# Chunk 4's last weight sum on VectorE instead of an accumulating DMA, and the residual written into PSUM by ScalarE ahead of the products

## The chip, the cores and the metric

The kernel runs on one core of a Trainium2 chip. The metric is the device time of one execution in microseconds (us). The engines are called PE (TensorE, matrix products), DVE (VectorE), ACT (ScalarE), POOL (GpSimd) and SP (SyncE, which only issues DMAs here). A profile is taken of one further execution, in which each instruction's start and duration are recorded.

## The reference

Two layers over 256 tokens of width 1024, float32 throughout. Each layer applies four residual steps, each followed by a layer norm with its own gain and bias:

```
x = layer_norm(x * ALPHA + 0.5 * swiglu(x, ffn1_gate, ffn1_up, ffn1_down))
x = layer_norm(x * ALPHA + mixer(x))          # gated conv, recurrence, pooling; w_in, w_out
x = layer_norm(x * ALPHA + cross_attn(x, mem, ca_q, ca_k, ca_v, ca_o))
x = layer_norm(x * ALPHA + 0.5 * swiglu(x, ffn2_gate, ffn2_up, ffn2_down))

swiglu(x, g, u, d) = (silu(x @ g) * (x @ u)) @ d       # g, u: 1024 x 2816, d: 2816 x 1024
```

ALPHA is a constant, the fourth root of 4. The comments name what each step holds; the mixer itself is not touched by the change.

## The kernel before

The tokens lie in two tiles of 128 (h, 128 x 1024 each); x transposed (xT) is PE's stationary or moving operand. Each weight is loaded as float32 into a 128 x 1024 buffer (raw, six of them), and split in two parts that PE multiplies at its fast rate: ACT rounds it to a high part (whi, L75), DVE subtracts to get the low part (wlo, L76). The eight buffers of each part turn over. A product is then three matmuls (mm_rows, L132): high by high, low by high, high by low.

A swiglu (called net here) has 2816 hidden columns, worked in five chunks of 512 (0 to 4) and one of 256 (5). For each, gate and up products go to PSUM banks of the kind acc; the hidden values are then gated, dealt to the other layout by small DMAs (dealt) and multiplied with the down weights, which adds up in four PSUM banks of the kind dn (two token tiles by two halves of the columns), over the whole net.

Some chunks, the sevens, compute the gate and up products by seven block products in place of eight (by_seven, L663 on): in the first net chunks 2 and 4, in the other three 2, 3, 4 and 5. For these, blocks of the weights are w00 and w10 (gate, first and second half of the rows) and w01 and w11 (up). The seven products take w00, w00 + w01, w10, w00 + w01 + w11, w01 + w11, w11 and last w00 + w01 + w11 + w10. Each sum that grows from w00 is made in w00's buffer in place. A sum by DVE is an instruction at L702 (raw<-raw). The last sum, to which w10 is added, is made before the change in two ways. For chunks of 512 (chunk 4 among them) POOL issues two accumulating DMAs, 512 KB each (the function more, L738), which read w10 from memory once more and add it to the buffer. For chunk 5 DVE adds w10's buffer. The sum w01 + w11 uses accumulating DMAs as well and stays as it is. At the end of a seven, DVE takes the bank called total into the hidden values (halves, L721); the last product of chunk 4 then writes that same bank, and so waits for it.

The homes of the blocks: w10 of a 512 chunk lies in spare2 and one raw buffer; chunk 5's w00 takes spare2 next. SP issues all plain loads in one queue in an order fixed by the scheduler, and an issue whose buffer is still in use holds up all behind it. lng and lnb are the norm's gain and bias, whose buffers sevens use as homes too.

At the end of each step finish (L328 on) makes for each tile the residual: h = h * ALPHA / scale + dn in two halves by DVE (L377, with the row sum as second result where the norm follows by ACT's squares), then the mean (L387), ACT's sum of squares (L392), rs (L398), the two norm operations (L407, L412) and PE's transposes (L199) for the next step.

Of the kernel before, what the change touches and what calls it, by code (L numbers as in the profile page):

```python
# [60 lines left out]
def model(ctx: ExitStack, tc: tile.TileContext, t: dict, out: bass.AP):  # L61
# [99 lines left out]
    def tok(i):  # L161
        return slice(i * P, (i + 1) * P)
# [162 lines left out]

    squares = kTh[:, 4:8, :].rearrange("p k c -> p (k c)")

    def finish(mm, y, scale, gb, units, last=False, junk=None, ahead=None, prompt=False):  # L328

        g, b = gb
        def later_split(i, j, unit):
            pt = acc((P, 4, P))
            for k in range(4):
                turns.append(nc.tensor.transpose(pt[:, k, :], h[i][:, (4 * j + k) * P : (4 * j + k + 1) * P], unit))
            dh, dl = (x[:, 4 * j : 4 * j + 4, tok(i)] for x in (xTh, xTl))
            nc.scalar.copy(dh, pt)  # L340
            return dh, dl, pt

        def turn_first():
            if prompt:
                held.extend(later_split(0, j, units[0]) for j in range(2))
            else:
                transposed(h[0], 0, xTh, xTl, units[0])

        def low_part(w):
            lows.append(nc.vector.tensor_tensor(w[1], w[2], w[0].bitcast(F32), op=ALU.subtract))  # L350

        held = []

        def tile_done(i):

            st = sm.tile([P, 4, 6], F32, tag="st", name="st")
            pieces, size = [slice(0, 512), slice(512, DM)], 512
            if last and i == NT - 1:

                pieces, size = [slice(0, 512), slice(512, 768), slice(768, DM)], 256  # L360
                c = slice(512, DM)
                v = halves(h[i][:, c])
                with tc.issue_after(lows[-1].ins):
                    nc.vector.scalar_tensor_tensor(v, v, ALPHA / scale, sums(y[i][1]), op0=ALU.mult, op1=ALU.add)
            for c in pieces:
                n = c.start // 512
                v = halves(h[i][:, c])
                if len(pieces) == 3 and n:
                    o = acc((P, 256))
                    mm(i, n, slice(c.start - 512, c.stop - 512), o, None)  # L370
                    nc.vector.tensor_tensor(v, v, sums(o), op=ALU.add)
                else:
                    mm(
                        i, n, slice(0, 512), None,
                        None if last or not i or not n else turn_first,
                    )
                    nc.vector.scalar_tensor_tensor(  # L377
                        v, v, ALPHA / scale, sums(y[i][n]), op0=ALU.mult, op1=ALU.add,
                        accum_out=None if junk is None else st[:, n, 0:1],
                    )  # L380
                for d in range(c.start, c.stop, size):
                    if junk is None:
                        nc.vector.bn_stats(st[:, d // size, :], h[i][:, d : d + size])
            mv = sm.tile([P, 2], F32, tag="mv", name="mv")
            rs = sm.tile([P, 1], F32, tag="rs", name="rs")
            if junk is not None:
                mean = nc.vector.tensor_scalar(  # L387
                    mv[:, 0:1], st[:, 0, 0:1], st[:, 1, 0:1], -1.0 / DM, op0=ALU.add, op1=ALU.mult
                )
                with ExitStack() as behind:  # L390
                    squared.append(
                        nc.scalar.activation(junk, h[i], AF.Square, bias=mv[:, 0:1], accum_out=mv[:, 1:2])  # L392
                    )
                    if prompt:
                        with tc.issue_after(mean.ins):
                            low_part(held.pop(0))
                        behind.enter_context(tc.issue_after(lows[-1].ins))
                    nc.vector.tensor_scalar(  # L398
                        rs, mv[:, 1:2], 1.0 / DM, LN_EPS / scale / scale, op0=ALU.mult, op1=ALU.add
                    )  # L400
            else:
                nc.vector.bn_aggr(mv, st[:, 0 : DM // size, :])
                nc.vector.tensor_scalar_add(rs, mv[:, 1:2], LN_EPS / scale / scale)
            nc.gpsimd.tensor_tensor(rs, rs, nhalf[:, 0:1], op=ALU.pow)
            cs = [slice(0, 512), slice(512, DM)]
            for c in cs:
                nc.vector.scalar_tensor_tensor(  # L407
                    h[i][:, c], h[i][:, c], mv[:, 0:1], g[:, c],
                    op0=ALU.subtract if junk is None else ALU.add, op1=ALU.mult,
                )  # L410
            for c in pieces:
                normed.append(nc.vector.scalar_tensor_tensor(  # L412
                    h[i][:, c], h[i][:, c], rs, b[:, c], op0=ALU.mult, op1=ALU.add
                ))
                if last:
                    e = nc.scalar if c.start == 512 else nc.sync
                    e.dma_start(out[0, tok(i), c], h[i][:, c])

        if ahead is None:
            tile_done(0)  # L420
            tile_done(1)
        else:
            split(*ahead.todo[0])
            if prompt:
                nc.scalar.copy(ahead.todo[1][0], ahead.todo[1][2])
                held.append(ahead.todo[1])
            with tc.issue_after(lows[-1].ins):
                tile_done(0)
            with tc.issue_after(normed[-1].ins):
                if prompt:  # L430
                    split(*ahead.todo[2])
                    split(*ahead.todo[3])
                tile_done(1)
                if not prompt:
                    for x in ahead.todo[1:]:
                        split(*x)
            if prompt:
                with tc.issue_after(normed[-1].ins):
                    low_part(held.pop())
        return lambda keep=None: transposed(h[1], 1, xTh, xTl, units[1], keep)  # L440

    def project_back(slabs, late, gb, scale, unit, between=lambda: None):


        y = [[acc((P, 512), "dn") for _ in range(2)] for _ in range(NT)]
        total = len(slabs)
        made = {}

        def mm(u, i, k, n):
            if u not in made:  # L450
                made[u] = slabs[u]()
            w, xh, xl = made[u]
            wh, wl = w.at(k, slice(n * 512, n * 512 + 512))
            mm_rows(
                y[i][n], xh[:, k, tok(i)], xl[:, k, tok(i)], wh, wl,
                u == 0 and k == 0, u == total - 1 and k == 1,
            )

        for u in range(total - late):
# [10 lines left out]
                for k in range(2):  # L470
                    mm(u, i, k, n)

        return finish(tail, y, scale, gb, (unit, unit), junk=squares if unit is pdn else None)


    def ffn(l, name, n, pend=None, last=False, early=None, started=None, following=None):
        gate, up, down = (t[f"{name}_{x}"][l] for x in ("gate", "up", "down"))
        with tc.tile_pool(name="ffn", bufs=2, reuse_waits="tile") as fp:
# [186 lines left out]
            def by_seven(c0, ncol, bx, between):  # L665
# [82 lines left out]
                activate(s, 0, o)  # L748
                w11 = block(up, 1, pieces(*homes[2]))
                run(total, bx[1], parts_of(w00, w11), True)  # L750
                if ncol == CHUNK:
                    more(w00, gate, 1)
                less = bank()
                copied = nc.scalar.mul(less, total, -1.0)
# [1 line left out]
                if ncol == CHUNK:  # L756
                    run(total, bx[2], parts_of(w01), True)
                    put(f, e, ALU.subtract, total)
                    run(less, bx[3], parts_of(w11), True)
                    run(total, part_of_x(1, 1), parts_of(w00), True)  # L760
                else:
                    run(less, bx[3], parts_of(w11), True)
                    run(total, bx[2], parts_of(w01), True)
# [65 lines left out]
            def rows_of(a, i, k, m, first, final, cols=slice(0, 512), alone=None):  # L829
                w, ah, al = a  # L830
                wh, wl = w.at(k, slice(m * 512 + cols.start, m * 512 + cols.stop))
                o = ys[i][m] if alone is None else alone
                mm_rows(o, ah[:, k, tok(i)], al[:, k, tok(i)], wh, wl, first, final)

            def both(c, u, a=None, steps=range(2)):
                a = a or slab(c, u)
                for i in range(NT):
                    for k in steps:
                        for m in range(2):
                            apart = last and i == m == k == u == 1 and c == 3  # L840
                            rows_of(a, i, k, m, c == u == k == 0, apart)

            todo = [(c, u) for c in range(4) for u in range(2)]
            later = (0, 0, 0, 0, 0, 0) if early is None else (0, 1, 0, 1, 0, 2)
            for c, (c0, ncol) in enumerate(chunks):
                if not c:
                    acts.append(first()())
                    ys = [[acc((P, 512), "dn") for _ in range(2)] for _ in range(NT)]
                elif c in sevens:
                    half = []  # L850

# [67 lines left out]
                        rows_of(a, i, k, m, first, u == 2 and k == 1, cols, alone)  # L919

            ahead = following() if following else None
            return ahead, finish(tail, ys, 0.5, gb, (idn, jdn) if name == "ffn1" else (pdn, pdn), last, None if last else squares, ahead, ahead is not None and name == "ffn1")

# [373 lines left out]
    def attention(l, pend):  # L1299
        scale = (DM // HEADS) ** -0.5  # L1300
        with tc.tile_pool(name="att", bufs=1, reuse_waits="tile") as ap:
# [19 lines left out]
            def weights(hh):  # L1321
                o = acc(tag="dn")
                for i in range(NT):
                    for d in (2 * hh, 2 * hh + 1):
                        mm_rows(
                            o[:, i, :], qTh[:, d, tok(i)], qTl[:, d, tok(i)], kTh[:, d, :], kTl[:, d, :],
                            d == 2 * hh, d != 2 * hh,
                        )
                mx = sm.tile([P, NT], F32, tag="mx", name="mx")
                nc.vector.tensor_reduce(mx, o, axis=AX.X, op=ALU.max)  # L1330
# [126 lines left out]
```

## Time and profile before

| | us |
|---|---|
| median of 3 runs | 1076.18 (1074.79 to 1076.83) |
| the profiled execution | 1078.4 |
| its span, first to last instruction | 1076.5 |
| granted TensorE clock, mean | 0.994 |

In the profile an L is a line of the kernel before; x counts instructions; out<-in are the names of the tiles. Where an engine was idle ahead of an instruction, brackets give the time and the engine and instruction that ended it. In the program after the change the same lines stand 11 to 15 further down (L702 becomes L713, L721 L732, L775 L787).

The four nets run at these times in the profile: layer 0's first from 0 to 150, its second from 365 to 541; layer 1's first from 541 to 705, its second from 905 to the end. The mixer and attention of layer 0 lie from 176 to 363, those of layer 1 from 704 to 905.

### The profile page before, as it was taken

To read this page: it belongs to the slowest core of one execution; us is meant where nothing else is said; L and a number is where in the kernel's file an instruction comes from. 1 tells how busy PE (TensorE), PEld (TensorE's weight loads), DVE (VectorE), ACT (ScalarE), POOL (GpSimd) and SP (SyncE) were. 2 spreads that over 40 slices of the span, in tenths; PEclk is the share of its full clock that TensorE was granted. 3 is DMA by queue.
4 is the path that set the end of the run, shared out by engine and by line. 5 is a ranking of instruction groups with operands and counts; after the bars stand their busy time and mean duration, and the time that the engine had idled before them with its cause. 6 is when DMAs were issued, how large, how long until landed. Compare 5 with 4: busy or idle time off the path is not lost.

```text
span 1076.5 us, 16511 instructions
## 1 busy us (share of the span) xinstructions
PE 1050.8 (98%) x5978; PEld 930.9 (86%) x5978; DVE 956.7 (89%) x1257; ACT 680.4 (63%) x936; POOL 110.0 (10%) x140
## 2 busy tenths in 40 slices
PE   9999999999999999998999998999999999999987
PEld 7888888989899888887888887998998998888876
DVE  6998898989989789998998998899899779889988
ACT  6675775676466557666657566676773657557661
POOL 8001001000000001110001101010000000011101
PEclk9999999999999999999999998999999999999999
DMA  9999985854676589998789999766646665899972
GB/s 364 290 297 296 256 276 158 260 175 122 224 262 208 175 263 269 265 280 251 247 274 278 279 274 258 257 226 226 204 131 217 213 234 172 261 284 275 260 233 69
DMA packets 145569, 257.35 MB, mean 239 GB/s; under 512 B 11440, under 2 KB 52176, under 8 KB 145488
## 3 DMA queue, kind: packets, MB, share of 16 engines
q1 hardware_dynamic: 130656, 228.89, 63.9%
q0 software_dynamic: 14256, 26.23, 14.2%
q10 hardware_dynamic: 576, 1.18, 0.3%
q8 instruction: 47, 0.77, 0.3%
q14 instruction: 34, 0.28, 0.1%
HBM read 240.80 MB, written 1.05 MB: 225 GB/s over the span
## 4 chain that ended last, share of the span: by engine, by line
PE 70%; issue 12%; DMA 8%; DVE 7%; ACT 2%; POOL 1%; DVEq 0%; POOLq 0%; SPq 0%; ACTq 0%
PE acc L132 44%; PE dn L132 23%; DMA raw<-in_ffn_gate_dram 6%; DVE wlo L76 3%; ACT whi L75 2%; DMA raw<-in_ffn_up_dram 2%; DVE raw L702 1%; PE acc L199 1%; POOL raw L738 1%; DVE halves L721 0%; PE dn L1135 0%; DMA raw<-in_ffn_down_dram 0%; DVE h L407 0%; DMA h<-in_x_dram 0%; PE dn L1209 0%
## 5 line engine op out<-in xcount | busy, mean ns | idle before, releaser
L76 DVE TENSOR_TENSOR wlo<-raw,whi 128x1024 fp32r<-128x1024 f32 (+1 forms) x470 | 552.0, 1208 | 47.6 <-ACT whi L75 42.8
L75 ACT CAST whi<-raw 128x1024 fp32r<-128x1024 f32 (+1 forms) x470 | 471.1, 1041 | 187.5 <-DVE raw L702 75.2
L132 PE MATMUL acc<-whi,xT 128*128 128x512 f32 (+1 forms) x944 | 282.2, 376 | 13.8 <-DVE halves L721 13.5
L132 PEld LDWEIGHTS acc<-whi,xT 128*128 128x128 f32 x944 | 178.4, 191 | 39.9 <-issue 13.2
L132 PE MATMUL acc<-wlo,xT 128*128 128x512 f32 (+1 forms) x472 | 176.9, 375 | 0.2 <-DVE wlo L76 0.2
L132 PE MATMUL dn<-whi,ah 128*128 128x512 f32 x346 | 130.3, 381 | 2.2 <-ACT whi L75 2.2
L132 PE MATMUL dn<-wlo,ah 128*128 128x512 f32 x346 | 131.2, 379 | 0.0
L132 PE MATMUL dn<-whi,al 128*128 128x512 f32 x346 | 131.1, 379 | 0.0
L132 PE MATMUL acc<-xT,whi 128*128 128x512 f32 x480 | 117.6, 381 | 0.0
L132 PEld LDWEIGHTS acc<-wlo,xT 128*128 128x128 f32 x472 | 90.5, 192 | 12.6 <-DVE wlo L76 0.6
L132 PEld LDWEIGHTS acc<-xT,whi 128*128 128x128 f32 x480 | 86.8, 190 | 9.8
L132 PE MATMUL dn<-whi,xT 128*128 128x512 f32 x288 | 87.7, 380 | 0.0
L132 PE MATMUL acc<-whi,kTh 128*128 128x512 f32 (+1 forms) x224 | 80.2, 358 | 0.0
L132 PE MATMUL acc<-wlo,kTh 128*128 128x512 f32 (+1 forms) x224 | 79.9, 357 | 0.0
L132 PE MATMUL acc<-whi,kTl 128*128 128x512 f32 (+1 forms) x224 | 79.9, 357 | 0.0
L132 PEld LDWEIGHTS dn<-whi,ah 128*128 128x128 f32 x346 | 65.2, 189 | 12.1 <-ACT whi L75 3.4
L132 PEld LDWEIGHTS dn<-whi,al 128*128 128x128 f32 x346 | 65.4, 189 | 9.2
L132 PEld LDWEIGHTS dn<-wlo,ah 128*128 128x128 f32 x346 | 65.4, 189 | 9.1 <-DVE wlo L76 0.3
L132 PEld LDWEIGHTS acc<-xT,wlo 128*128 128x128 f32 x480 | 62.9, 191 | 3.2
L702 DVE TENSOR_TENSOR raw<-raw 128x1024 f32<-128x1024 f32 x53 | 63.8, 1216 | 0.2
L132 PE MATMUL acc<-xT,wlo 128*128 128x256 f32 x480 | 63.2, 275 | 0.0
L132 PEld LDWEIGHTS dn<-whi,xT 128*128 128x128 f32 x288 | 54.4, 189 | 7.5
(250 smaller groups left out, 1339.5 us busy)
## 6 DMA issues: line engine op xcount, KB each, us to landing
raw<-in_ffn_up_dram SPq DMA_DIRECT2D x88, 512.0 KB, 6.1
raw<-in_ffn_down_dram SPq DMA_DIRECT2D x88, 512.0 KB, 5.9
raw<-in_ffn_gate_dram SPq DMA_DIRECT2D x84, 512.0 KB, 6.0
raw<-in_w_in_dram SPq DMA_DIRECT2D x48, 512.0 KB, 4.7
raw<-in_ffn_up_dram POOLq DMA_DIRECT2D x25, 512.0 KB, 6.3
raw<-in_ffn_gate_dram POOLq DMA_DIRECT2D x22, 512.0 KB, 9.1
dealt<-sg SPq DMA_DIRECT2D x80, 128.0 KB, 4.6
raw<-in_ca_k_dram SPq DMA_DIRECT2D x16, 512.0 KB, 5.1
```

What stands on the lines that cost most here:

```text
L75: rounded = nc.scalar.copy(hi, src)
L76: lows.append(nc.vector.tensor_tensor(lo, src, hi.bitcast(F32), op=ALU.subtract))
L132: turns.append(nc.tensor.matmul(o, w, x, start=start, stop=stop, skip_group_check=more))
L199: turns.append(nc.tensor.transpose(pt[:, k, :], src[:, (4 * j + k) * P : (4 * j + k + 1) * P], unit))
L702: nc.vector.tensor_tensor(r[i], r[i], plus[i], op=ALU.add)
L738: nc.gpsimd.dma_start(x, part_of(m, j, i), accum_op=ALU.add)
```

## The change

Chunk 4 in the three nets with four sevens: the two accumulating DMAs for w00 are gone, and DVE adds w10 from its buffer (two instructions of 128 x 1024, L713 after), as in chunk 5. In chunk 2 and 3, and in the first net, the DMA stays. The w10 buffers are used until these adds.

Seeds: for the second net of layer 0, the first of layer 1 and both attention outputs, ACT writes h * ALPHA / scale into the four dn banks before the first product (the function seed, four instructions per step, 16 in all), and the products add to them, with no start flag. finish then has ACT read each bank (Identity, with the row sum as second result) into h, 16 instructions, where DVE had the residual sum.

In the attention weights one start flag per bank is left, with no change of work.

```diff
+    def seed(y, scale):
+        for i in range(NT):
+            for n in range(2):
+                nc.scalar.mul(sums(y[i][n]), halves(h[i][:, n * 512 : n * 512 + 512]), ALPHA / scale)
...
-                    nc.vector.scalar_tensor_tensor(
-                        v, v, ALPHA / scale, sums(y[i][n]), op0=ALU.mult, op1=ALU.add,
-                        accum_out=None if junk is None else st[:, n, 0:1],
-                    )
+                    if seeded:
+                        nc.scalar.activation(v, sums(y[i][n]), AF.Identity, accum_out=st[:, n, 0:1])
+                    else:
...
+        seeded = unit is pdn
+        if seeded:
+            seed(y, scale)
...
-                if ncol == CHUNK:
+                by_transfer = ncol == CHUNK and (len(sevens) < 4 or c0 != 4 * CHUNK)
+                if by_transfer:
                     more(w00, gate, 1)
...
-                    run(total, part_of_x(1, 1), parts_of(w00), True)
+                    run(total, part_of_x(1, 1), parts_of(w00, None if by_transfer else w10), True)
...
-                            rows_of(a, i, k, m, c == u == k == 0, apart)
+                            rows_of(a, i, k, m, c == u == k == 0 and not seeded, apart)
...
+                    seeded = early is None and not last
+                    if seeded:
+                        seed(ys, 0.5)
```

DVE's order at the end of chunk 4 in the second net of layer 0. Before (raw_4731 and raw_4732 are w00 of chunk 4, raw_4980 is w00 of chunk 5):

```order
L76 TENSOR_TENSOR wlo_4959<-raw_4731,whi_4958 128x1024
L76 TENSOR_TENSOR wlo_4963<-raw_4732,whi_4962 128x1024
L76 TENSOR_TENSOR wlo_4991<-raw_4980,whi_4990 128x1024
L702 TENSOR_TENSOR raw_4980<-raw_4980,raw_4982 128x1024
L721 TENSOR_TENSOR halves_4744<-halves_4744,acc_4746 128x512
L76 TENSOR_TENSOR wlo_5009<-raw_4980,whi_5008 128x1024
L721 TENSOR_TENSOR halves_4744<-halves_4744,acc_4879 128x512
L76 TENSOR_TENSOR wlo_5027<-raw_4984,whi_5026 128x1024
L76 TENSOR_TENSOR wlo_5047<-raw_5042,whi_5046 128x1024
L76 TENSOR_TENSOR wlo_5051<-raw_5043,whi_5050 128x1024
L702 TENSOR_TENSOR raw_4980<-raw_4980,raw_5067 128x1024
L775 TENSOR_TENSOR sg_4743<-sg_4743,halves_4744 128x1024
```

After (raw_4739 and raw_4740 are w00 of chunk 4, raw_4747 and raw_4748 w10, raw_4988 w00 of chunk 5):

```order
L713 TENSOR_TENSOR raw_4739<-raw_4739,raw_4747 128x1024
L713 TENSOR_TENSOR raw_4740<-raw_4740,raw_4748 128x1024
L76 TENSOR_TENSOR wlo_4966<-raw_4739,whi_4965 128x1024
L76 TENSOR_TENSOR wlo_4971<-raw_4740,whi_4970 128x1024
L732 TENSOR_TENSOR halves_4752<-halves_4752,acc_4754 128x512
L732 TENSOR_TENSOR halves_4752<-halves_4752,acc_4885 128x512
L76 TENSOR_TENSOR wlo_4999<-raw_4988,whi_4998 128x1024
L713 TENSOR_TENSOR raw_4988<-raw_4988,raw_4990 128x1024
L787 TENSOR_TENSOR sg_4751<-sg_4751,halves_4752 128x1024
L76 TENSOR_TENSOR wlo_5017<-raw_4988,whi_5016 128x1024
L76 TENSOR_TENSOR wlo_5035<-raw_4992,whi_5034 128x1024
L76 TENSOR_TENSOR wlo_5055<-raw_5050,whi_5054 128x1024
```

The two adds stand ahead of the subtractions, both halves ahead of chunk 5's first subtraction, and the long product (L775, after L787) behind the first sum of chunk 5 and no longer behind the second.

SP's loads for chunk 5 in the same net, before (raw_4980 is w00, raw_4982 w01, raw_4984 w10, raw_5067 w11):

```order
L685 DMA raw_4980<-in_ffn2_gate_dram 128x4x256
L685 DMA raw_4982<-in_ffn2_up_dram 128x4x256
L685 DMA raw_4984<-in_ffn2_gate_dram 128x4x256
L98 DMA raw_5042<-in_ffn2_down_dram 128x1024
L98 DMA raw_5043<-in_ffn2_down_dram 128x1024
L321 DMA lng_5156<-in_ln_g_dram 128x1024
L322 DMA lnb_5157<-in_ln_b_dram 128x1024
L685 DMA raw_5067<-in_ffn2_up_dram 128x4x256
L98 DMA raw_5175<-in_ffn2_down_dram 128x1024
```

and after (raw_4988 is w00, raw_4990 w01, raw_4992 w10, raw_5075 w11):

```order
L696 DMA raw_4990<-in_ffn2_up_dram 128x4x256
L696 DMA raw_4992<-in_ffn2_gate_dram 128x4x256
L98 DMA raw_5050<-in_ffn2_down_dram 128x1024
L321 DMA lng_5164<-in_ln_g_dram 128x1024
L322 DMA lnb_5165<-in_ln_b_dram 128x1024
L696 DMA raw_4988<-in_ffn2_gate_dram 128x4x256
L98 DMA raw_5051<-in_ffn2_down_dram 128x1024
L696 DMA raw_5075<-in_ffn2_up_dram 128x4x256
L98 DMA raw_5183<-in_ffn2_down_dram 128x1024
```

w00 was the first of these and is now behind w01, w10, a down load, lng and lnb, at the place that w11 had.

ACT's order from behind the squares of the first tile to the second net's first gate, at the end of layer 0's attention, before:

```order
L75 CAST whi<-raw 128x1024 x2
L75 CAST xT<-acc 128x4x128 x2
L75 CAST whi<-raw 128x1024 x4
L392 ACTIVATE kTh,mv<-h_73,mv 128x1024
L510 ACT_TABLE_LOAD
L510 ACTIVATE sg<-acc 128x512
L75 CAST xT<-acc 128x4x128 x2
```

and after (dn<-h are seeds for the net, h_73,st<-dn reads of the second tile's banks):

```order
L331 ACTIVATE dn<-h_72 128x2x256
L75 CAST whi<-raw 128x1024
L75 CAST xT<-acc 128x4x128 x2
L75 CAST whi<-raw 128x1024 x3
L383 ACTIVATE h_73,st<-dn 128x512
L75 CAST whi<-raw 128x1024
L400 ACTIVATE kTh,mv<-h_73,mv 128x1024
L75 CAST whi<-raw 128x1024
L331 ACTIVATE dn<-h_72 128x2x256
L521 ACT_TABLE_LOAD
L521 ACTIVATE sg<-acc 128x512
L331 ACTIVATE dn<-h_73 128x2x256 x2
```

The reads of tile 1 stand among the casts of weights, and the seeds around the table load and the Silu of the first chunk.

On PE, 81 second-half products (dn) now stand behind the last product of chunk 5 into acc in each of these nets, where it was 84; the difference stands ahead of it.

More of the change, by code (lines that the diff above doesn't have):

```diff
@@ L326, in model, with finish @@
     squares = kTh[:, 4:8, :].rearrange("p k c -> p (k c)")
-    def finish(mm, y, scale, gb, units, last=False, junk=None, ahead=None, prompt=False):
+    def seed(y, scale):
+        for i in range(NT):
+            for n in range(2):
+                nc.scalar.mul(sums(y[i][n]), halves(h[i][:, n * 512 : n * 512 + 512]), ALPHA / scale)
+    def finish(mm, y, scale, gb, units, last=False, junk=None, ahead=None, prompt=False, seeded=False):
         g, b = gb
@@ L376, in tile_done @@
                     )
-                    nc.vector.scalar_tensor_tensor(
-                        v, v, ALPHA / scale, sums(y[i][n]), op0=ALU.mult, op1=ALU.add,
-                        accum_out=None if junk is None else st[:, n, 0:1],
-                    )
+                    if seeded:
+                        nc.scalar.activation(v, sums(y[i][n]), AF.Identity, accum_out=st[:, n, 0:1])
+                    else:
+                        nc.vector.scalar_tensor_tensor(
+                            v, v, ALPHA / scale, sums(y[i][n]), op0=ALU.mult, op1=ALU.add,
+                            accum_out=None if junk is None else st[:, n, 0:1],
+                        )
                 for d in range(c.start, c.stop, size):
@@ L455, in mm @@
                 y[i][n], xh[:, k, tok(i)], xl[:, k, tok(i)], wh, wl,
-                u == 0 and k == 0, u == total - 1 and k == 1,
+                u == 0 and k == 0 and not seeded, u == total - 1 and k == 1, seeded,
             )
@@ L471, in tail @@
                     mm(u, i, k, n)
-        return finish(tail, y, scale, gb, (unit, unit), junk=squares if unit is pdn else None)
+        return finish(tail, y, scale, gb, (unit, unit), junk=squares if seeded else None, seeded=seeded)
     def ffn(l, name, n, pend=None, last=False, early=None, started=None, following=None):
@@ L921, in ffn @@
             ahead = following() if following else None
-            return ahead, finish(tail, ys, 0.5, gb, (idn, jdn) if name == "ffn1" else (pdn, pdn), last, None if last else squares, ahead, ahead is not None and name == "ffn1")
+            return ahead, finish(tail, ys, 0.5, gb, (idn, jdn) if name == "ffn1" else (pdn, pdn), last, None if last else squares, ahead, ahead is not None and name == "ffn1", seeded)
     def key_weights(l, c, hold=False):
@@ L1326, in weights @@
                             o[:, i, :], qTh[:, d, tok(i)], qTl[:, d, tok(i)], kTh[:, d, :], kTl[:, d, :],
-                            d == 2 * hh, d != 2 * hh,
+                            i == 0 and d == 2 * hh, d != 2 * hh, True,
                         )
```

2 lines of the change are left out of this document (1 added, 1 removed).

## The prediction

> **What bounds the kernel now.** I began with the share of busy time (the columns are busy us, share of the span and instructions).
>
> ```profile
> PE 1050.8 (98%) x5978; PEld 930.9 (86%) x5978; DVE 956.7 (89%) x1257; ACT 680.4 (63%) x936; POOL 110.0 (10%) x140
> ```
>
> TensorE (PE) is the bound, and time can only be won where it stands still. Next, the waits of PE over the whole span, and the chain of waits where the longest lies, in the first ffn of layer 1.
>
> ```profile
> PE acc L132 <- DVE halves L721: 13.5, 4, 4.5
> ```
>
> ```profile
> 647.92 11.55 DMA raw<-in_ffn_gate_dram
> 659.49 1.05 ACT whi L75
> ...
> 661.71 1.23 DVE wlo L76
> 662.96 1.22 DVE raw L702
> 664.18 0.61 DVE halves L721
> 664.93 5.46 PE acc L132 x12
> ```
>
> PE's largest wait, 13.5 us in four places, is for VectorE (DVE) to have read a bank that the next product overwrites (halves, L721). Behind it stands a transfer of 11.55 us, the accumulating one of chunk 4. The other two nets with four sevens show the same transfer:
>
> ```profile
> 478.50 10.75 DMA raw<-in_ffn_gate_dram
> ```
>
> ```profile
> 1012.81 11.03 DMA raw<-in_ffn_gate_dram
> ```
>
> The windows (PE, weight loads, DVE, ACT and POOL busy, then granted clock, DMA share and GB/s) show what the wait costs in layer 1's first ffn.
>
> ```profile
> 610.00:660.00 50.00, 50.00 (x233) 43.59 (x232) 46.16 (x44) 32.42 (x38) 7.18 (x6) 1.00 1.03 285
> 660.00:664.00 4.00, 0.41 (x2) 0.00 (x1) 3.40 (x3) 1.48 (x2) 0.00 (x0) 0.96 0.85 307
> 664.00:670.50 6.50, 5.57 (x14) 4.52 (x15) 5.93 (x8) 3.96 (x5) 1.29 (x1) 0.50 0.63 101
> ```
>
> PE is empty for 4 us and is then granted half the clock for 6.5 us. But DVE's column is the one to read: 46.16 of 50 us busy ahead of the wait and 5.93 of 6.5 behind it. The change removes the wait by giving DVE more to do just there, so the gain is bounded by DVE's idle time, not by PE's. That idle time, in the timeline of DVE, the row of that wait from each net in order of time (in the first with the halves that PE waits for):
>
> ```profile
> 490.35 2.36 DVE L76 TENSOR_TENSOR wlo<-raw,whi 128x1024 fp32r<-128x1024 f32 x2 [1.89 <-ACT whi L75]
> ...
> 493.89 0.68 DVE L721 TENSOR_TENSOR halves<-halves,acc 128x512 f32<-128x512 f32 x1
> ```
>
> ```profile
> 660.57 2.36 DVE L76 TENSOR_TENSOR wlo<-raw,whi 128x1024 fp32r<-128x1024 f32 x2 [2.68 <-ACT whi L75]
> ```
>
> ```profile
> 1024.94 2.36 DVE L76 TENSOR_TENSOR wlo<-raw,whi 128x1024 fp32r<-128x1024 f32 x2 [2.16 <-ACT whi L75]
> ```
>
> and, from the waits of DVE in the some 20 us behind each (us in total, times, longest):
>
> ```profile
> DVE wlo L76 <- ACT whi L75: 1.7, 2, 1.1
> ```
>
> ```profile
> DVE wlo L76 <- ACT whi L75: 3.6, 3, 1.9
> ```
>
> ```profile
> DVE wlo L76 <- ACT whi L75: 2.4, 3, 1.1
> ```
>
> So DVE idles 1.89 + 1.7 = 3.59 us, 2.68 + 3.6 = 6.28 us and 2.16 + 2.4 = 4.56 us in the three stretches. Behind each, PE runs from a store of second-half products and DVE no longer matters.
>
> **The change part by part: chunk 4's sum.** Six accumulating transfers go, and six DVE adds come. Their kind is there already:
>
> ```profile
> L702 DVE TENSOR_TENSOR raw<-raw 128x1024 f32<-128x1024 f32 x53 | 63.8, 1216 | 0.2
> ```
>
> ```profile
> 482.70 5.76 DVE L76 TENSOR_TENSOR wlo<-raw,whi 128x1024 fp32r<-128x1024 f32 x5
> ```
>
> Five operations of this size take 5.76 us together, so they follow each other every 1.14 us; two adds cost 2.28 us per net. The fifth of these, from 487.25 on, subtracts for the half of w00 whose transfer came in time; the other half is the row at 490.35. In the new order the adds stand at 487.25 and 488.39, the two subtractions follow at 489.5 and 490.7 with their casts hidden beside them, then both halves operations. They end at about 493.1, and PE may go on at about 492.6, where now the halves (0.68 us from 493.89) end at 494.6. PE's wait falls to about 2 us. Nothing is gained yet: what decides is when DVE is through with chunk 5.
>
> There three things change. First, of the three sums of chunk 5, the first had half a wait (1.7 - 1.1 = 0.6 us), the second none, the third this one:
>
> ```profile
> 508.41 2.36 DVE L76 TENSOR_TENSOR wlo<-raw,whi 128x1024 fp32r<-128x1024 f32 x2 [1.11 <-ACT whi L75]
> ```
>
> It is the time in which ACT casts a sum just made, with nothing else for DVE to do. In the new order the long product of sg stands behind the first sum and no longer behind the second, so two sums of three show this wait: 2 x 1.11 = 2.22 us. Second, 3 of PE's second-half products move ahead of the end of chunk 5 (81 remain behind it, 84 before): worth 3 x 0.216 = 0.65 us, by the spacing of
>
> ```profile
> 659.59 0.38 PE L132 MATMUL acc<-whi,kTh 128*128 128x512 f32 x1
> 659.81 0.38 PE L132 MATMUL acc<-wlo,kTh 128*128 128x512 f32 x1
> ```
>
> Third, and least known: chunk 5's w00 goes into the buffer that w10 now holds until the first add ends, at 487.25 + 1.22 = 488.5. On SP's queue it stands where now the up weights of chunk 5 are issued, behind lng and lnb:
>
> ```profile
> 488.49 0.38 SPq L685 DMA_DIRECT2D raw<-in_ffn_up_dram  x1
> ```
>
> The same issue in the three nets (KB, us to landing), and the median of another 512 KB load:
>
> ```profile
> raw<-in_ffn_up_dram SPq DMA_DIRECT2D x1, 512.0 KB, 6.2
> ```
>
> ```profile
> raw<-in_ffn_up_dram SPq DMA_DIRECT2D x1, 512.0 KB, 5.8
> ```
>
> ```profile
> raw<-in_ffn_up_dram SPq DMA_DIRECT2D x1, 512.0 KB, 5.1
> ```
>
> ```profile
> raw<-in_w_in_dram SPq DMA_DIRECT2D x48, 512.0 KB, 4.7
> ```
>
> With t us from issue to landing and a cast of 1.05 us, DVE can take w00 at 488.5 + t + 1.1, and is free at 493.1: it waits t - 3.5 us. The upper end is the 6.2 of today, a wait of 2.7. The lower end is no wait (t up to 3.5). The accumulating transfers no longer run beside it, 1 MB per net, so I take the three rows less 1.4 us: 4.8, 4.4 and 3.7, around the 4.7 of the quieter load; waits of 1.3, 0.9 and 0.2. Each tenth in t moves the sum by 0.3.
>
> The Trainium skill, page "DMA: Bandwidth & Descriptors", section "Anatomy of one DMA", gives 2.0 us plus bytes over 436 GB/s for a transfer issued from GpSimd; my estimate by it for 512 KB is 3.2 us. The trace differs: no row above is below 4.7. By the page the wait would be nil, and the first rival below would be the forecast.
>
> Sum for chunk 4 and 5 (idle now, less adds, less sums' waits, less w00, plus products): 3.59 - 2.28 - 2.22 - 1.3 + 0.65 = -1.6 us; 6.28 - 2.28 - 2.22 - 0.9 + 0.65 = +1.5; 4.56 - 2.28 - 2.22 - 0.2 + 0.65 = +0.5. Together +0.4 us gained. The 2 accumulating transfers on POOL's queue hide nobody else's work, and what they fetched lies in SBUF already. The half clock goes, but DVE sets the pace there, so it isn't counted again.
>
> The Trainium skill, page "Perfetto Trace Analysis", section "Optimizing Scalar/DVE Operations", holds that a saturated DVE should hand work to Scalar. The first part of this change does the reverse. By the rule alone six adds would cost 6.8 us; the trace has DVE idle inside these stretches, so the sum nets one against the other.
>
> **The seeds and the finish.** DVE loses 16 residual sums:
>
> ```profile
> L377 DVE SCALAR_TENSOR_TENSOR h<-h,dn 128x512 f32<-128x512 f32 x31 | 21.1, 681 | 15.1 <-PE dn L132 15.1
> L377 DVE DVE_READ_ACCUMULATOR h<-h,dn 128x1 f32 x20 | 1.6, 82 | 0.0
> ```
>
> 16 x 0.76 = 12.2 us off DVE. I give PE nothing for it: DVE waits for PE 15.1 us in front of these very sums, and PE has no wait at the stage joints in its list. ACT gains 16 seeds and 16 reads out of PSUM of 512 columns, nearest
>
> ```profile
> L1009 ACT COPY v<-acc 128x512 f32<-128x512 f32 x4 | 2.4, 604 | 6.3 <-PE acc L132 6.3
> ```
>
> about 0.6 us each; the seeds could cost less if a write to PSUM is quicker, or a table load more. ACT is 63% busy. The last joint before ffn2 of layer 0 shows what hides this:
>
> ```profile
> 367.85 1.17 ACT L392 ACTIVATE kTh<-h,mv 128x1024 fp32r<-128x1024 f32 x1
> ```
>
> ```profile
> 371.29 1.41 DVE L412 SCALAR_TENSOR_TENSOR h<-h,rs,lnb 128x512 f32<-128x512 f32 x2
> ```
>
> ```profile
> 372.83 1.04 PE L199 MATMUL acc<-pdn,h 128*128 128x128 f32 x8
> ```
>
> The second tile's squares (L392) follow ACT's casts, the norm ends at 372.70 and PE transposes at 372.83, without a pause before. One read of 0.6 us in ACT's queue, less 0.1 to 0.2 for a residual sum that starts no later, would shift the norm by 0.3 to 0.45 us, and PE has other products queued. I take 0.05 per finish, 0.2 us in all; bounds are nothing and 0.4 each, 1.6 in all. The seeds themselves stand behind the Silu of the next gate and ahead of tile 1's casts; PE has its first chunk's products meanwhile. The start flags of the attention weights cost nothing.
>
> Total: 0.4 - 0.2 = 0.2 us gained, 1078.2 for the profiled execution of 1078.4. The profile lies 2.2 us above the median of the runs, 1076.18, so the forecast is 1076.0.
>
> **The rivals.** *Early load.* w00 lands within 3.5 us, without the traffic of the accumulating transfers, and DVE doesn't wait: 2.4 us more, 1073.6. The rows of 4.7 and more speak against it, the DMA share of 1.03 ahead of the stretch, which falls, for it. Chance 0.17. *DVE was the bound at the joints too.* A third of the 12.2 us reaches PE, through casts and subtractions of the next stage's first chunks that come earlier: 1076.0 - 4.1 = 1071.9. Against it: PE has no listed wait there. For it: DVE is 89% busy and PE's small waits may be averaged away. Chance 0.13. *Late load, slower.* w00 waits behind lng, lnb and a down load and needs today's 6.2 us in all nets: waits of 2.7 x 3 = 8.1 instead of 2.4, 1081.7; from about 5 us in all three (4.5 of wait, 2.1 more) the kernel is slower by over 0.2%. Chance 0.14. *ACT late at the finishes, slower.* Its reads queue behind casts, or bring a table load each time,
>
> ```profile
> L510 ACT ACT_TABLE_LOAD x4 | 5.1, 1283 | 0.1
> ```
>
> of 1.28 us: four finishes x 1 us past the cover is 1080.0; it decides above 0.6 us each. Chance 0.08.
>
> **How the numbers follow.** A measurement of this kernel tells apart about 0.2%, 2.15 us. The forecast has 0.48; its own range, by a few tenths in t, is 1073.8 to 1078.0 and lies within 0.2% but for its ends: faster 0.08, same 0.35, slower 0.05. The early load adds 0.12 to faster and 0.05 to same, the joints 0.13 to faster, the two slower rivals 0.19 to slower and 0.03 to same. In all faster 0.33, same 0.43, slower 0.24. The range reaches to the joints' rival below and between the slower ones above: 1071.0 to 1080.0.
>
> **What would show it.** In the new profile: PE's wait for halves falls from 13.5 us to about 6 over the three nets (and chunk 2's) with a clock of 1.00 behind it; DVE shows raw sums at about 487 and 488; a wait of 0.2 to 1.3 us before chunk 5's first subtraction, and two of 1.1 us behind; no table loads beside the seeds. The forecast is wrong if DVE has no such waits, if PE waits at a joint, or if the stretches from chunk 2 to chunk 4 move.

## The result and the profile after

The changed kernel takes 1084.18 us (median of 4 runs, 1083.21 to 1085.15) where the kernel before takes 1076.51 beside it (4 runs). The ratio is 1.0069, with a 95% interval of 1.005 to 1.0087: slower by 7.4 us. The ratios here and in the table below are estimated from the single executions and not from the two medians, whose quotient differs by up to 0.0017 and lies within each interval; three executions far outside (2859.51 us of the kernel before, 5698.48 and 1851.34 us of two variants) are left out of them. The span of the profiled execution grew from 1076.5 to 1083.2 us, at a mean granted clock of 0.995 for 0.994.

The transposes at the joints show where. The last ones ahead of layer 0's second net start at 372.61 (372.83 before); all joints up to there are 0.2 us early, from the first at 171.81 (172.04 before) on. From there to the next joint 4.1 us are lost, over layer 1's first net 1.7, over the mixer and attention behind it nothing, and over the last net 1.1. These are the three nets with chunk 4's new adds; the seeds lie at joints, where PE has no wait before or after the change.

The longest waits of PE in the kernel after (us in total, times, longest):

```profile
PE acc L132 <- DVE halves L732: 5.0, 3, 1.7
PE dn L132 <- ACT whi L75: 3.5, 3, 1.3
PE acc L132 <- ACT whi L75: 3.0, 4, 0.8
PE acc L132 <- DVE wlo L76: 2.7, 4, 0.9
PE acc L132 <- ACT acc L753: 2.5, 3, 0.8
```

The wait for halves fell from 13.5 to 5.0 us, 1.7 in each net. Three others stand behind it (the third to the fifth row), together 8.2 us, where before there were 0.4, 0.2 and none. In two of them PE waits for the parts of weights, in the third for ACT's copy of a bank (L753). The chain of waits in the second net of layer 0 shows why:

```profile
486.36 1.23 DVE wlo L76
487.58 1.15 DVE raw L713
488.73 0.02 issue
488.75 5.76 DMA raw<-in_ffn_gate_dram
494.50 0.02 issue
494.52 0.02 ACTq L75
494.54 0.04 issue
494.58 1.05 ACT whi L75
495.64 0.02 issue
495.66 1.24 DVE wlo L76
```

The first add (L713) frees the buffer of w10, chunk 5's w00 is then loaded into it, and cast and subtraction follow. This load is on the path, as the accumulating transfer was before. DVE's timeline at that place:

```profile
487.49 2.36 DVE L713 TENSOR_TENSOR raw<-raw 128x1024 f32<-128x1024 f32 x2
489.84 2.37 DVE L76 TENSOR_TENSOR wlo<-raw,whi 128x1024 fp32r<-128x1024 f32 x2
492.12 1.47 DVE L732 TENSOR_TENSOR halves<-halves,acc 128x512 f32<-128x512 f32 x2
495.66 1.23 DVE L76 TENSOR_TENSOR wlo<-raw,whi 128x1024 fp32r<-128x1024 f32 x1 [2.06 <-ACT whi L75]
```

The adds stand where the prediction put them (487.49 for 487.25), the halves end at 493.6 for its 493.1, and then DVE idles 2.06 us. In the other two nets this wait is 1.74 and 2.67 us. The load from issue to landing, one row from each net in order:

```profile
raw<-in_ffn_gate_dram SPq DMA_DIRECT2D x1, 512.0 KB, 5.8
```

```profile
raw<-in_ffn_gate_dram SPq DMA_DIRECT2D x1, 512.0 KB, 5.4
```

```profile
raw<-in_ffn_gate_dram SPq DMA_DIRECT2D x1, 512.0 KB, 6.3
```

DVE's waits over the whole stretch of chunks 4 and 5 in the three nets (3.59, 6.28 and 4.56 before):

```profile
DVE wlo L76 <- ACT whi L75: 4.3, 3, 2.1
DVE both L732 <- PE acc L132: 0.5, 1, 0.5
```

```profile
DVE wlo L76 <- ACT whi L75: 4.0, 3, 1.7
DVE both L732 <- PE acc L132: 0.5, 1, 0.5
```

```profile
DVE wlo L76 <- ACT whi L75: 4.9, 3, 2.7
```

DVE has six adds more (6.8 us) and still idles 14.2 us, where it idled 14.4: waits and adds together grew by 6.6 us, and the span by 6.7. Net by net the two agree less well (3.5, 0.5 and 2.6 us more on DVE, 4.1, 1.7 and 1.1 us lost), so it is partly luck that the totals come out so close. The adds didn't fill the idle time, they pushed it on to the next load.

At the joints the change did what it says at no price. ACT's groups of the new operations:

```profile
L383 ACT ACTIVATE h<-dn 128x512 f32<-128x512 f32 x16 | 9.6, 601 | 19.4 <-PE dn L132 19.4
L331 ACT ACTIVATE dn<-h 128x512 f32<-128x512 f32 x16 | 9.3, 614 | 0.9 <-DVE h L420 0.8
L383 ACT ACTIVATION_READ_ACCUMULATOR h<-dn 128x1 f32 x16 | 3.2, 199 | 0.0
```

Reads of 0.60 and seeds of 0.61 us, as estimated, with 0.20 us more per read for its row sum (the last line), and no table load was added.

### The profile page after: what moved, and what is told of

It is laid out like the page before. It is cut to its first block, busy times and chain, and to the rows that moved or that the text cites. A ratio compares the mean times of both kernels' runs of the same rounds, so it can differ in the third digit from the quotient of the medians.

```text
span 1083.2 us, 16502 instructions
## 1 busy us (share of the span) xinstructions
PE 1054.9 (97%) x5978; PEld 929.8 (86%) x5978; DVE 953.9 (88%) x1231; ACT 699.2 (65%) x984; POOL 102.2 (9%) x134
## 4 chain that ended last, share of the span: by engine, by line
PE 78%; DVE 8%; DMA 6%; ACT 4%; issue 3%; SPq 0%; DVEq 0%; POOL 0%; ACTq 0%
PE acc L132 53%; PE dn L132 23%; DVE wlo L76 5%; ACT whi L75 3%; DMA raw<-in_ffn_up_dram 2%; DMA raw<-in_ffn_gate_dram 2%; DMA raw<-in_ffn_down_dram 1%; PE acc L199 1%; DVE raw L713 1%; DVE square L542 1%; DMA dealt<-both 1%; PE dn L1150 0%; DVE al L76 0%; PE dn L1224 0%; DVE both L787 0%
## 5 line engine op out<-in xcount | busy, mean ns | idle before, releaser
L132 PEld LDWEIGHTS dn<-wlo,ah 128*128 128x128 f32 x346 | 65.7, 190 | 13.5 <-DVE wlo L76 4.6
L132 PEld LDWEIGHTS dn<-whi,ah 128*128 128x128 f32 x346 | 65.4, 190 | 13.5 <-ACT whi L75 4.9
L713 DVE TENSOR_TENSOR raw<-raw 128x1024 f32<-128x1024 f32 x59 | 71.0, 1220 | 0.3
L749 POOL DMA_DIRECT2D raw<-in_ffn_up_dram x25 | 30.3, 1212 | 345.1 <-DVE raw L713 121.1
```

The costliest lines, as they stand in the source:

```text
L132: turns.append(nc.tensor.matmul(o, w, x, start=start, stop=stop, skip_group_check=more))
L713: nc.vector.tensor_tensor(r[i], r[i], plus[i], op=ALU.add)
L749: nc.gpsimd.dma_start(x, part_of(m, j, i), accum_op=ALU.add)
```

## The experiments

Theory A: the loss is the late landing of chunk 5's w00, which waits for the first add and then for what is queued ahead of it on SP. Rival B: it is ScalarE's new work. Rival C: it is the six adds themselves, on an engine without idle time. Each ratio is against the kernel before, run on the same chip in the same session. The two kernels with short adds leave out nearly all of w10 in chunk 4's last sum.

| kernel | median us | before | ratio, 95% interval |
|---|---|---|---|
| the change | 1084.18 | 1076.51 | 1.0069 (1.0050 to 1.0087) |
| chunk 4 alone | 1081.52 | 1077.70 | 1.0052 (1.0030 to 1.0073) |
| seeds alone | 1077.40 | 1077.70 | 1.0007 (0.9985 to 1.0029) |
| short adds | 1076.61 | 1077.70 | 1.0001 (0.9981 to 1.0021) |
| buffers exchanged | 1076.94 | 1077.70 | 1.0004 (0.9986 to 1.0022) |
| lng, lnb behind | 1079.78 | 1077.56 | 1.0019 (1.0002 to 1.0036) |
| exchanged, lng, lnb behind | 1077.67 | 1077.56 | 0.9999 (0.9983 to 1.0015) |
| exchanged, no seeds | 1078.37 | 1077.56 | 1.0002 (0.9990 to 1.0015) |
| exchanged, w00 late | 1086.51 | 1077.56 | 1.0075 (1.0053 to 1.0097) |
| short adds, w00 late | 1084.14 | 1077.50 | 1.0070 (1.0053 to 1.0087) |
| exchanged and refilled | 1071.61 | 1077.50 | 0.9954 (0.9940 to 0.9969) |
| before, refilled | 1076.11 | 1077.50 | 0.9999 (0.9983 to 1.0015) |
| exchanged, refilled, no seeds | 1072.24 | 1076.87 | 0.9962 (0.9948 to 0.9977) |

**Which part.** Chunk 4 alone leaves out the seeds:

```diff
-        seeded = unit is pdn
+        seeded = False
...
-                    seeded = early is None and not last
+                    seeded = False
```

> The changed kernel without the seeds: chunk 4's last weight sum by VectorE, the residual by VectorE at the finish as before. Theory A (the loss lies in chunk 4 and 5 of the three nets, where chunk 5's first weight block now lands late): as slow as the whole change, 1083 to 1085 us. Rival B (the loss is ScalarE's work for the seeds and reads): within 1 us of the kernel before, about 1076.5.

Seeds alone keeps the transfers:

```diff
-                by_transfer = ncol == CHUNK and (len(sevens) < 4 or c0 != 4 * CHUNK)
+                by_transfer = ncol == CHUNK
```

> The kernel before with the seeds and ScalarE's reads alone; chunk 4's sum by the accumulating transfers as before. Theory A: within 1 us of the kernel before (the joints between the stages moved by nothing in the trace), 1075.5 to 1077.5 us. Rival B: 1083 to 1085.

Chunk 4 alone is slow by 0.52%, somewhat under the range but inside the interval of the whole change; the seeds alone make no difference. B falls.

**The adds or the load.** The first try cut the adds from 1024 columns to two:

```diff
+                            c = plus[i].shape[-1]
+                            nc.vector.tensor_tensor(r[i][:, :, 0:c], r[i][:, :, 0:c], plus[i], op=ALU.add)
...
-                    run(total, part_of_x(1, 1), parts_of(w00, None if by_transfer else w10), True)
+                    run(total, part_of_x(1, 1), parts_of(w00, None if by_transfer else [x[:, :, 0:1] for x in w10]), True)
```

> The changed kernel with the adds of all weight sums that take the w10 block in chunk 4 cut to two columns of 1024 (chunk 4's last product then lacks w10): VectorE is free of 6 x 1.14 = 6.8 us, but w10's buffer is held as long, and chunk 5's first block is still issued behind lng. Theory A: VectorE waits for that load instead, and at most 3 us are won, 1081 to 1084. Rival C (the six adds themselves are the loss, on an engine without idle time): 1076 to 1078.

1.0001: theory A's number was missed and C's met. The trace said why this didn't separate them. Without the long add in front w00 is issued 0.2 us behind the first add's start and no longer 1.3, and the scheduler had put lnb behind it (lng stayed ahead, issued 1.2 us before). It then took, in the three nets:

```profile
raw<-in_ffn_gate_dram SPq DMA_DIRECT2D x1, 512.0 KB, 4.2
```

```profile
raw<-in_ffn_gate_dram SPq DMA_DIRECT2D x1, 512.0 KB, 4.4
```

```profile
raw<-in_ffn_gate_dram SPq DMA_DIRECT2D x1, 512.0 KB, 5.3
```

The edit had shortened the adds and the load at once. So the load was held at its place with short adds: lng and lnb are issued ahead of chunk 5's w00, as in the changed kernel, and DVE's order is the same.

```diff
+                with ExitStack() as behind:
+                    if ncol < CHUNK:
+                        behind.enter_context(tc.issue_after(gains[-1].ins))
+                    w00 = block(gate, 0, pieces(*homes[0]))
...
+                    if c == 5:
+                        gb = ln_params(l, n)
                     left = by_seven(
...
-                if c == 5:
+                if c == 5 and len(sevens) < 4:
```

> The adds cut to two columns again (chunk 4's last product then lacks w10), and w00 issued behind both lng and lnb, as in the changed kernel; VectorE's order is the changed kernel's. Theory A (the path runs from the first add over w00's issue and the queue to VectorE): w00 is issued at most 1.1 us earlier than in the changed kernel and lands about 6 us later, so VectorE idles for it longer and at most half of the 6.8 us of adds is won: 1079 to 1082. Rival C (the adds alone are the loss): 1076 to 1078, as with the short adds before.

1.0070, as slow as the change with all its adds. A had expected up to half of the adds to come back, 1079 to 1082 us; none did. DVE's timeline:

```profile
487.98 2.36 DVE L77 TENSOR_TENSOR wlo<-raw,whi 128x1024 fp32r<-128x1024 f32 x2 [1.04 <-ACT whi L76]
495.67 1.22 DVE L77 TENSOR_TENSOR wlo<-raw,whi 128x1024 fp32r<-128x1024 f32 x1 [3.95 <-ACT whi L76]
```

What the adds gave up became idle time (3.95 us for 2.06, and 1.04 in front). Counted from the second tile's transposes ahead of the net (372.28 here, 372.61 in the changed kernel), w00 was issued 1.2 us earlier, at 487.24, but landed at 494.52, 0.3 us later than in the changed kernel, and its subtraction began 0.3 us later too. SP's issues of lng, lnb and w00 (at 486.48, 487.61 and 488.75 in the changed kernel), and the load:

```profile
485.68 0.34 SPq L322 DMA_DIRECT2D lng<-in_ln_g_dram  x1
486.82 0.33 SPq L323 DMA_DIRECT2D lnb<-in_ln_b_dram  x1
487.24 0.39 SPq L697 DMA_DIRECT2D raw<-in_ffn_gate_dram  x1
```

```profile
raw<-in_ffn_gate_dram SPq DMA_DIRECT2D x1, 512.0 KB, 7.3
```

C falls: while w00 is late, the adds cost nothing. Issuing the load earlier behind the same two transfers did not make it land earlier, so its landing is fixed by the queue ahead of it.

**Taking the lateness away, adds and all.** The buffers of w00 and w11 are exchanged in chunk 5; w11 is needed last.

```diff
-                    homes = [("spare2",), ("raw",), ("raw",), ("raw",)]
+                    homes = [("raw",), ("raw",), ("spare2",), ("raw",)]
```

> The changed kernel with the homes of two of chunk 5's blocks exchanged: w00 into a raw buffer, w11 (needed last) into spare2. All instructions and adds stay; w00 is issued ahead of lng and lnb again. Theory A: the three waits for w00 (2.06, 1.74 and 2.67 us) go, with the half clock behind the first two, 1076.5 to 1079. Rival C: no change, 1083 to 1085.

1.0004: w00 is issued at 472.57, ahead of lng and lnb, its wait is gone in all three nets, and the loss with it. The same kernel with w00 put behind lng and lnb (the lines of the diff before last, on top of the exchange; w01 and w10 move back with it):

> The exchange of buffers, but with w00 (and behind it w01 and w10) issued behind lng and lnb on purpose; the adds, the instructions and the buffers are those of the exchange, and VectorE's order that of the changed kernel. Theory A (lateness of w00 is the larger part of the loss): slow again, 1082 to 1087. Rival C, or if the exchange helped by something else than the time of the load: 1076 to 1079.

1.0075. Adds, instructions and buffers are those of the exchange, DVE's order is that of the changed kernel, and 0.7% comes back with the place of these loads. DVE's wait for w00, 2.70, 3.60 and 1.87 us in the three nets (its other waits there are 1.1 to 1.3 us for sums and one of 0.36):

```profile
496.67 1.23 DVE L77 TENSOR_TENSOR wlo<-raw,whi 128x1024 fp32r<-128x1024 f32 x1 [2.70 <-ACT whi L76]
```

The milder cure leaves w00 in its buffer and only moves lng and lnb behind chunk 5's blocks:

```diff
                 if c == 5:
-                    gb = ln_params(l, n)
+                    with tc.issue_after(loads[-1].ins):
+                        gb = ln_params(l, n)
```

> The changed kernel with the norm's gain and bias (lng, lnb) issued behind chunk 5's weight blocks: w00 keeps its buffer and waits for the first add as before, but two transfers of 512 KB no longer stand right ahead of it. Theory A (w00 comes late because it waits for the first add and then for what is queued ahead): its 5.4 to 6.4 us from issue to landing fall to about 4.2, VectorE's waits for it from 6.5 us in all to 1 to 3, time 1078 to 1081. Rival C (only the six adds count): no change, 1083 to 1085.

1.0019, and 1079.78 us, within the 1078 to 1081 that A gave. The load takes 3.6, 3.7 and 3.7 us from issue to landing, and DVE waits 0.70, 0.85 and 0.84 us for it. The load and the wait in the first of the three nets:

```profile
raw<-in_ffn_gate_dram SPq DMA_DIRECT2D x1, 512.0 KB, 3.6
```

```profile
494.34 1.23 DVE L76 TENSOR_TENSOR wlo<-raw,whi 128x1024 fp32r<-128x1024 f32 x1 [0.70 <-ACT whi L75]
```

Two more runs ask whether something is left beside w00, with both cures together, and with the exchange but no seeds:

> Both repairs together: w00 in a raw buffer, issued early, and lng and lnb behind chunk 5's blocks. Theory A: no wait for w00 is left to shorten, so within 1 us of the exchange of buffers alone, 1075.5 to 1078. If other loads of chunk 5 still set the pace: 2 us or more below it.

> The exchange of buffers (w00 in a raw buffer, w11 in spare2) without the seeds: chunk 4's sum by VectorE alone. Theory A (seeds and reads move nothing): 1076 to 1078, as with them. Rival B (the seeds cost or gain at the joints): more than 2 us apart from it.

0.9999 and 1.0002: moving lng and lnb as well gains nothing more, and neither do the seeds.

**What the adds can be worth.** With w00 in time, DVE's waits are three per net of 1.1 to 1.2 us, each while ACT casts a sum just made (3.5, 3.4 and 3.4 us). In chunk 5 the next block's split is now made between a sum and the sum's own split:

```diff
+                if narrow:
+                    grow(w00, w01)
+                    p10 = parts_of(w10)
+                run(one, bx[0], parts_of(w00, None if narrow else w01))
...
+                if narrow:
+                    grow(w00, w11)
+                    p11 = parts_of(w11)
+                run(total, bx[1], parts_of(w00, None if narrow else w11), True)
```

> The exchange of buffers, and in chunk 5 the next block's subtraction put between each of the first two sums and the sum's own subtraction, so that VectorE has work while ScalarE casts the sum. Theory A (VectorE's waits in chunk 5 are PE's loss one for one): two of three waits of 1.1 us per net go, 6 us in three nets, 1070 to 1074. If PE is held up by the later products instead: 1076 to 1078, as the exchange alone.

0.9954, 5.0 us faster than the kernel before. DVE in the stretch:

```profile
493.15 1.22 DVE L711 TENSOR_TENSOR raw<-raw 128x1024 f32<-128x1024 f32 x1
494.29 2.51 DVE L76 TENSOR_TENSOR wlo<-raw,whi 128x1024 fp32r<-128x1024 f32 x2
...
504.79 1.22 DVE L711 TENSOR_TENSOR raw<-raw 128x1024 f32<-128x1024 f32 x1
507.12 1.23 DVE L76 TENSOR_TENSOR wlo<-raw,whi 128x1024 fp32r<-128x1024 f32 x1 [1.11 <-ACT whi L75]
```

Of nine waits three are left, where the scheduler put the subtraction ahead of the sum. The same refilling on the kernel before:

> The kernel before (accumulating transfers, no seeds) with the same refilling of chunk 5. Theory A: VectorE's waits of 0.6 to 1.9 us in chunk 5 shrink, but chunk 4's stall for the transfer (3.7, 4.7 and 4.2 us of PE) stays: 1072 to 1076. The refilled exchange is ahead of it by 0 to 4 us, by what chunk 4's adds are worth once nothing waits behind them.

0.9999, and 1076.11 us, just above the range's 1076: PE still waits 11.4 us for halves, and DVE idles 14.6 us in these stretches, as much as in the kernel before (14.4): the wait for the accumulating transfer takes what the refilling freed. So it pays only once the transfer is off the path, and the adds pay only once DVE's waits are refilled.

Last, the refilled exchange without the seeds:

> The refilled exchange without the seeds: VectorE makes the residual at the finish again. Theory A (nothing at the joints bounds the kernel): equal to the refilled exchange with seeds within its interval, 1070.5 to 1073. If the seeds' relief of VectorE counts once chunk 5 waits less: 1073.5 or more.

0.9962, inside the other's interval. The seeds are worth nothing that these runs can tell apart, in any of three pairs of kernels (the kernel before, the exchange and the refilled exchange, each with and without). In a fourth, the change (1.0069) and chunk 4 alone (1.0052), the intervals overlap; without the seeds w00 took 5.1, 5.5 and 5.5 us there, and DVE waited 1.4 us less for it in all. The fastest median is that of the refilled exchange, 1071.61 us.

## Why the prediction was wrong

It forecast 1076.0 us and a range up to 1080.0.

**What bounds the kernel: right.** DVE's idle time and not PE's wait for halves decided: that wait fell by 8.5 us, and nothing came of it.

**The adds: right in place and price** (487.49 and on, 1.14 us apart), and w00's wait was the right thing to ask about: t - 3.5 gives 2.25, 1.9 and 2.85 us for the landing times measured, and DVE waited 2.06, 1.74 and 2.67.

**The failed step is t itself.** The prediction took the rows of today's load in that slot "less 1.4 us: 4.8, 4.4 and 3.7", since the accumulating transfers no longer run beside it. Measured were 5.8, 5.4 and 6.3, on average what the up weights took there (6.2, 5.8 and 5.1). The traffic beside it was the wrong cause, and the trace of before shows that there was little of it: the accumulating transfers end at 489.25, 659.47 and 1023.84 (start and duration in the prediction's rows), and the up load is issued at 488.49, 657.91 and 1022.80, so the two overlap for 0.8 to 1.6 us only. The experiments name the right cause, the transfers queued ahead on SP: with lng and lnb behind it the same load took 3.6 to 3.7 us, with lng alone ahead 4.2 to 5.3, with both ahead 5.4 to 6.3 (5.1 to 5.5 in chunk 4 alone), and issued 1.2 us earlier behind both it landed no earlier. The prediction had this at hand: the load stood "behind lng and lnb". Measured waits are 4.1 us over the 2.4 of the sum.

**Two smaller terms.** The 0.65 us per net for 3 products that move ahead seem not to have been won: behind chunk 5 PE now waits for subtractions of the down weights, 1.4 us in the three nets,

```profile
PE dn L132 <- DVE wlo L76: 1.4, 3, 0.8
```

No run separates this term. And DVE has a wait of 0.5 us for PE (both, L732) in two nets, which the sum lacked. 4.1 + 3 x 0.65 + 1.0 is 7.1 us, less the 0.2 forecast as gain 6.9; the span grew by 6.7. This is an account of the sum's terms and not a proof of each, and as it doesn't hold net by net (above), its closeness is partly luck.

**The sums' waits: right,** 1.17 and 1.11 us in the trace for the 1.11 predicted twice per net. **The seeds: right,** PE waits at no joint, and the runs with and without seeds can't be told apart. The prediction put one piece of advice too strongly: of a saturated DVE the Trainium skill, page "Perfetto Trace Analysis", section "Optimizing Scalar/DVE Operations", says only that offloading some work to Scalar "may make sense", and the 16 residual sums handed over here brought nothing that the runs show.

**The rivals.** The late load was among them, with its mechanism, but at 6.2 us in all nets and 1081.7 us, and with a chance of 0.14. Its waits for w00 were too long (8.1 us for 6.5), and its price came out too low all the same, by the products and both. The early load, the joints and ACT at the finishes didn't happen. The exchange is the early load made to happen, by another buffer: no wait for w00 is left, and still it takes 1.0004 and not the 0.998 of that rival's 1073.6 us, and one reason is that DVE has three waits of 1.1 to 1.2 us per net for its sums there, where the prediction had two. The estimate of 3.2 us from the Trainium skill (page "DMA: Bandwidth & Descriptors", section "Anatomy of one DMA", for a transfer issued from GpSimd) comes near SP's load where SP had issued nothing for 6.8 us ahead of it, 3.6 to 3.7 us; that section has no term for the queue in front, which decided.

What stays open: adds plus waits of DVE in the three stretches, against the 14.4 us of the kernel before, give the time by the ratio to within 1 us for nine of the thirteen kernels. The exchange (17.1 us, with lng and lnb moved or without seeds too) came out 2.3 to 2.8 us better than that account, and the kernel with lng and lnb behind (20.1 us) 3.7 us better. Why is not shown. In these four the second halves operation stands behind w00's subtraction, but it does so in the refilled exchange too, which fits the account.

## What to carry to other kernels

When work is moved off a transfer onto an engine, look at what the engine's operands still hold: a buffer kept until the adds moved the next load from the front of its queue behind five others, two of them right ahead of it, and that load became the path. Price a load by what is queued ahead of it on its issuing engine, and not by a median or by traffic that may be over when it is issued. Extra work on a nearly full engine can pay, but here only after that engine's own small waits had been given something to do.

## What the runs showed of the hardware

The time from issue to landing of one 512 KB load went from 3.6 us to 8.0 with its place in SP's queue (7.1 to 7.7 with short adds and w00 late, 6.3 to 8.0 with the exchange and w00 late). From none to lng to lng and lnb ahead, each of these 512 KB transfers went with 0.6 to 1.6 us more, 1.1 on average, though other loads moved as well; and a load issued 1.2 us earlier behind the same transfers landed no earlier. The Trainium skill, page "DMA: Bandwidth & Descriptors", section "Two DMAs through the same engine are not ordered", has descriptors of one queue start in order on each DMA engine; that agrees.

The granted clock fell without any long pause of PE. The windows of the kernel after in layer 0's second net (PE, weight loads, DVE, ACT and POOL busy, then granted clock, DMA share and GB/s):

```profile
491.00:494.00 3.00, 1.43 (x7) 0.98 (x6) 2.49 (x4) 0.00 (x0) 0.00 (x0) 1.00 0.85 276
494.00:497.00 3.00, 2.12 (x11) 1.46 (x9) 1.31 (x2) 1.64 (x2) 0.00 (x0) 1.00 1.06 379
497.00:500.00 3.00, 1.81 (x12) 1.43 (x12) 3.00 (x3) 1.82 (x2) 1.29 (x1) 1.00 0.23 87
500.00:506.00 6.00, 5.51 (x29) 5.31 (x30) 5.02 (x5) 4.00 (x7) 0.00 (x0) 0.72 1.00 188
```

PE's longest wait here is 1.6 us, but it is busy for only 5.4 of 9 us in several pieces, and then gets a clock of 0.72 over 6 us, where the prediction expected 1.00. Before, with one wait of 3.6 us at this place, the clock stayed at 1.00. The busy share doesn't decide it either. With short adds and w00 late PE is busy for less, and the clock stays at 1.00:

```profile
494.00:500.00 6.00, 2.25 (x13) 1.68 (x13) 4.29 (x4) 3.35 (x4) 1.29 (x1) 1.00 0.51 191
500.00:506.00 6.00, 5.50 (x37) 5.13 (x37) 5.04 (x5) 3.90 (x7) 0.00 (x0) 1.00 0.99 192
```

With the exchange and w00 late PE is busy for 5.5 of the 9 us, and the clock is 1.00 too. So these runs show no rule for when the clock falls.

The clock is not the cause of the loss. The mean granted clock of the profiled executions is 0.994 in the kernel before, 0.995 in the changed one, and 0.997 with short adds and w00 late, which is as slow. Nor is it the cause of the refilling's gain: the exchange and the refilled exchange ran at 0.998 to 0.999 alike, and are 0.5% apart.
